# Moving one activation tile by 448 bytes and running three short passes once, in a two-layer encoder trunk

## The chip, the cores and the metric

The kernel runs on one core of one Trainium2 chip. The metric is the device time of one execution in microseconds. Before the change the median of three runs is 2716.47 us (2715.73 to 2719.71).

## The reference, cut to what matters

The trunk takes 256 tokens of width 2048 and puts 16 learned tokens ahead of them. Layer 0 is a state-space mixer and a SwiGLU feed-forward; then one shared K and V is projected; layer 1 is a stick-breaking attention and a second SwiGLU feed-forward; a final norm follows and the 16 tokens are dropped. Everything is float32. The part that the change touches is this:

```python
def swiglu(u, w_gate_up, w_down):
    gu = u @ w_gate_up
    return (jax.nn.silu(gu[..., :FFN_HIDDEN]) * gu[..., FFN_HIDDEN:]) @ w_down
...
h = h + swiglu(rmsnorm(h, norm_ffn[layer]), ffn_gate_up[layer], ffn_down[layer])
```

FFN_HIDDEN is 5632, so a feed-forward multiplies by a 2048 x 11264 and a 5632 x 2048 matrix. In layer 1 only the 256 tokens that are returned go through it.

## The kernel before

**How the work is tiled.** Activations lie transposed: 128 partitions carry 128 features, the free dimension carries tokens, and a tensor of width 2048 is 16 blocks k. Each output tile of 128 features by 256 (or 272) tokens is one accumulation in a PSUM bank over all k. TensorE holds a 128x128 piece of the weight matrix and streams the tokens of block k past it.

**Three passes for one product.** Each float32 operand is split into two float32r halves, a rounded one and the remainder. ScalarE casts the rounded weights `hi` (line 101), VectorE subtracts to get `lo` (line 103). `mac` (lines 107 to 112) then issues three passes per k: hi with the rounded activation (line 110), hi with the activation's remainder (111), lo with the rounded activation (112). A pass is one load of a 128x128 weight piece into the array and one matmul; the weights are loaded anew for each pass.

**Activation tiles.** A tile such as `u` has the shape [128, 16, 2, tokens]: for each k the rounded half and then the remainder. With 256 tokens each half is 1024 bytes per partition, so all halves of a tile begin at the same distance from a multiple of 512 (and of 1024). In the program as it is allocated the second feed-forward's input `u` (made at line 596 in a slot that the inputs of the earlier stages used before it) begins at byte 26,624 of each partition, which is 52 x 512. The query projection's input `uq` begins at 126,400, which is 246 x 512 + 448, the output projection's input `ob` at 159,168 (310 x 512 + 448), and the second feed-forward's hidden tile `hid` again at 126,400. All slots of `hi` and `lo` begin at multiples of 4096, and a 128x128 piece in them is 512 bytes per partition.

**Order of the work.** The order is written out by hand; each engine runs its own list, and semaphores connect them. `project` (line 114) makes one output tile in two halves of 8 k each: it issues the load of 512 KB of weights on SyncE's queue (five slots), the cast, the subtraction, and 24 passes. `project_block` (line 130) does the same for several output tiles at once, so that all of them run over the first 8 k before any needs the second 8.

**The second feed-forward.** `ffn` (line 472) makes the first four tiles (gate 0, up 0, gate 1, up 1) with `project_block`. Between its two halves stands `rstd` (line 165): one float32 matmul of the squared sums with a matrix of ones into the bank `pr`, a square root on ScalarE and a reciprocal on VectorE, which give the norm's factor `r`. Then the loop over 44 blocks m takes gate tile and up tile, from the four finished ones first and with `project` from m = 2 on; each is scaled by `r` (line 145), the gate goes through SiLU, the product is split into `hid`. The down projection follows: four tiles with `project_block`, twelve with `project`.

The lines around the tile are these; `finish_o` fills `u` while the attention's output projection runs, so the last matmuls on `ob` are followed directly by the first on `u`:

```python
u = upool.tile([P, KD, 2, SEQ], F32R, tag="u", name="u2")

def finish_o(m, ps):
    hm = h[:, m, META:]
    residual(hm, ps)
    split_scaled(u, m, hm, gam[:, 3, m:m + 1])
```

In the profile, u2 and the earlier tiles of that slot are all called u; those with 256 columns are u2.

Of the kernel before, what the change touches and what calls it, by code (L numbers as in the profile page):

```python
# [6 lines left out]
F32 = mybir.dt.float32  # L7
F32R = mybir.dt.float32r
# [5 lines left out]
P = 128  # L14
D = 2048
KD = D // P
SEQ = 256
# [25 lines left out]
def trunk(tc, a, out):  # L43
    nc = tc.nc
    V, S, PE = nc.vector, nc.scalar, nc.tensor

    with tc.tile_pool(name="const", bufs=1) as cp, \
# [38 lines left out]
        def nm(s):  # L86
            uid[0] += 1
            return f"{s}_{uid[0]}"


        def load(src, k0, n, m=P):
            raw = wp.tile([P, LC, P], F32, tag="raw", name=nm("raw"), bufs=RAW)
            b0 = k0 // LC * LC
            b1 = min(b0 + LC, src.shape[0] // (P * m))
            piece = src[b0 * P * m:b1 * P * m].rearrange("(p k c) -> p k c", p=P, c=m)
            nc.sync.dma_start(raw[:, :n, :m], piece[:, k0 - b0:k0 - b0 + n, :])
            return raw

        def halves(raw, n, m=P):
            hi = wp.tile([P, WC, P], F32R, tag="hi", name=nm("hi"), bufs=5)  # L100
            S.copy(hi[:, :n, :m], raw[:, :n, :m])  # L101
            lo = wp.tile([P, WC, P], F32R, tag="lo", name=nm("lo"), bufs=4)
            V.tensor_tensor(out=lo[:, :n, :m], in0=raw[:, :n, :m],  # L103
                            in1=hi[:, :n, :m].bitcast(F32), op=ALU.subtract)
            return hi, lo

        def mac(ps, hi, lo, j, x, k, first, last, m=P):
            n = x.shape[-1]
            wh, wl, xh, xl = hi[:, j, :m], lo[:, j, :m], x[:, k, 0, :], x[:, k, 1, :]
            PE.matmul(ps[:, :n], wh, xh, start=first, stop=False)  # L110
            PE.matmul(ps[:, :n], wh, xl, start=False, stop=False)  # L111
            PE.matmul(ps[:, :n], wl, xh, start=False, stop=last)  # L112

        def project(src, x, m=P, o=None, then=None):
            K = x.shape[1]
            if o is None:
                o = pp.tile([P, 512], F32, tag="pp", name=nm("pp"))
            o = o[:m]
            for k0 in range(0, K, WC):
                c = min(WC, K - k0)  # L120
                if k0 % LC == 0:
                    raw = load(src, k0, min(LC, K - k0), m)
                hi, lo = halves(raw[:, k0 % LC:], c, m)
                for j in range(c):
                    mac(o, hi, lo, j, x, k0 + j, k0 + j == 0, k0 + j == K - 1, m)
                if k0 == 0 and then:
                    then()
            return o

        def project_block(srcs, x, then=None):  # L130
            K = x.shape[1]
            pss = [pp.tile([P, 512], F32, tag="pp", name=nm("pp")) for _ in srcs]
            for k0 in range(0, K, WC):
                c = min(WC, K - k0)
                for ps, src in zip(pss, srcs):
                    hi, lo = halves(load(src, k0, c), c)
                    for j in range(c):
                        mac(ps, hi, lo, j, x, k0 + j, k0 + j == 0, k0 + j == K - 1)
                    pump()
                if k0 == 0 and then:  # L140
                    then()
            return pss

        def times(dst, ps, r):
            V.tensor_tensor(out=dst, in0=ps[:, :r.shape[-1]], in1=r, op=ALU.mult)  # L145
# [19 lines left out]
        def rstd(dst, acc, width, more=()):  # L165
            n = acc.shape[-1]
            ps = prp.tile([P, 512], F32, tag="pr", name=nm("pr"))
            parts = [acc, *more]
            for i, part in enumerate(parts):
                PE.matmul(ps[:, :n], ones, part, start=i == 0, stop=i == len(parts) - 1)  # L170
            sd = sp.tile([P, T], F32, tag="ms", name=nm("sd"), bufs=1)[:, :n]
            S.activation(sd, ps[:, :n], AF.Sqrt, bias=epst, scale=1.0 / width)
            V.reciprocal(dst, sd)
# [14 lines left out]
        u = upool.tile([P, KD, 2, T], F32R, tag="u", name="u0")  # L188
# [4 lines left out]
        for k, c in PIECES:  # L193
# [11 lines left out]
            hi, lo = halves(raw, GT * c)  # L205
# [6 lines left out]
        with tc.tile_pool(name="ssd0", bufs=1) as q0, \  # L212
# [13 lines left out]

            with tc.tile_pool(name="dtp", bufs=1) as dq:
                psd = project(a["w_dt"], u, m=NH, o=ptp.tile([P, 512], F32, tag="pt", name=nm("pt")),
                              then=lambda: rstd(rB, acc, D))[:, :T]
                for j in range(GT):  # L230
# [3 lines left out]
                def ahead(ct):  # L234
                    early[ct] = project(a["w_in"][32 + ct], u, o=pyp.tile([P, 512], F32, tag="py", name=nm("pe")))
# [37 lines left out]
                for b, (b0, b1) in enumerate(BLK):  # L273
                    n = b1 - b0
                    PE.transpose(pt[:n, b * NH:(b + 1) * NH], cum[:, b0:b1], ident[:NH, :NH])
                    PE.transpose(pt[:n, (3 + b) * NH:(4 + b) * NH], dt[:, b0:b1], ident[:NH, :NH])
                for b, (b0, b1) in enumerate(BLK):
                    n = b1 - b0
# [189 lines left out]
            u = upool.tile([P, KD, 2, T], F32R, tag="u", name="u1")  # L468
            out_project(6, u)


        def ffn(layer, u, t0, finish):
            n = T - t0
            with tc.tile_pool(name=f"ffn{layer}", bufs=1) as fp, \
                    tc.tile_pool(name=f"fft{layer}", bufs=2) as ft:
                hid = fp.tile([P, KF, 2, n], F32R, name=f"hid{layer}")
                gu, dn = a["w_gu"][layer], a["w_down"][layer]
                r = rB[:, t0:]
                pre = project_block([gu[0], gu[KF], gu[1], gu[KF + 1]], u,
                                    lambda: rstd(r, acc[:, t0:], D))  # L480
                for m in range(KF):
                    gt = ft.tile([P, n], F32, tag="gt", name=nm("gt"))
                    times(gt, pre.pop(0) if pre else project(gu[m], u), r)
                    S.activation(gt, gt, AF.Silu)
                    ut = ft.tile([P, n], F32, tag="ut", name=nm("ut"))
                    times(ut, pre.pop(0) if pre else project(gu[KF + m], u), r)
                    V.tensor_tensor(out=ut, in0=ut, in1=gt, op=ALU.mult)
                    S.copy(hid[:, m, 0, :], ut)
                    V.tensor_tensor(out=hid[:, m, 1, :], in0=ut, in1=hid[:, m, 0, :].bitcast(F32),
                                    op=ALU.subtract)  # L490
                for i, ps in enumerate(project_block([dn[m] for m in range(FILLERS)], hid)):
                    finish(i, ps)
                for m in range(FILLERS, KD):
                    finish(m, project(dn[m], hid))
# [3 lines left out]
        def finish0(m, ps):  # L498
# [4 lines left out]
            sumsq(acc, h[:, m, :], m == 0)  # L503

        ffn(0, u, 0, finish0)
        ukv = ukv[0]


        with tc.tile_pool(name="att1", bufs=1) as b1p, \
# [68 lines left out]
            pre = project_block([a["w_kv"][0], a["w_kv"][KD]], ukv, lambda: rstd(rB, acc, D))  # L578
# [14 lines left out]
                next(heads[m])  # L593
            side.extend(heads[-2:])

            u = upool.tile([P, KD, 2, SEQ], F32R, tag="u", name="u2")

            def finish_o(m, ps):
                hm = h[:, m, META:]
# [11 lines left out]
        def finish1(m, ps):  # L611
# [7 lines left out]
            if m == KD - 2:  # L619
                S.activation(warm, acc[:, META:META + 1], AF.Sqrt)  # L620

        ffn(1, u, META, finish1)


# [9 lines left out]
        pr = pp.tile([P, 512], F32, tag="pp", name="prow")  # L634
# [3 lines left out]
        m = 0  # L638
        for n in (1, 3, 4, 4, 4):
            o = wp.tile([P, LC, P], F32, tag="raw", name=nm("o"), bufs=RAW)  # L640
            o = o.rearrange("p k c -> p (k c)")[:, :n * SEQ].rearrange("p (k t) -> p k t", t=SEQ)
# [53 lines left out]
def build(shapes):  # L695
    import concourse.bacc as bacc

    nc = bacc.Bacc("TRN2", target_bir_lowering=False, num_devices=1, dynamic_dma_scratch_size=1024)
    a = {n: nc.dram_tensor(n, s, F32, kind="ExternalInput").ap() for n, s in shapes.items()}
    out = nc.dram_tensor("out", (P, KD, SEQ), F32, kind="ExternalOutput").ap()  # L700
    with tile.TileContext(nc) as tc:
        trunk(tc, a, out)
    return nc
# [11 lines left out]
```

## Time and profile before

| | |
|---|---|
| median of three runs | 2716.47 us |
| the profiled execution | 2715.76 us |
| its span | 2714.0 us |
| mean granted TensorE clock | 0.998 |
| TensorE busy, passes | 2700.6 us, 22112 |
| VectorE busy | 1605.6 us (59%) |
| ScalarE busy | 1307.1 us (48%) |
| DMA, mean | 177 GB/s |

The span runs from the first to the last instruction of one execution. Matmuls overlap: one that is listed with 280 ns begins some 115 ns after the one before it, so the pace of a stage is read from the starts or from the number of matmuls in a stretch of time, and not from the duration of one. A row of the grouped view has the line, the engine, the operation, the tile written and the tiles read, shapes, count, busy time in us and mean duration in ns; behind a second bar stands the idle time ahead of these instructions and what ended it. PE is TensorE's matmul, PEld its weight load, ACT ScalarE, DVE VectorE. In the row of a window stand its bounds in us, its length, the busy time and the number of instructions of the chosen engine, the granted clock, the DMA engines' busy share and GB/s.

### The profile page before, as it was taken

The page shows a single profiled execution, that of the slowest core. Times are in us where ns is not written, and L with a number is a line of the kernel's source. Part 1 is how long each engine was busy: PE and PEld are TensorE (multiplying, and loading weights), DVE is VectorE, ACT ScalarE, POOL GpSimd, SP SyncE. Part 2 cuts the span into 40 slices and gives each one's busy share as a digit, 9 for nine tenths or more (in the row PEclk, how much of TensorE's full clock was granted, in tenths as well). Part 3 has the DMA queues.
Part 4 walks back from the last instruction along what each step waited for, and adds up shares of the span by engine and source line. Part 5 has one row for each costly group of instructions (what it writes and reads, how often), then busy time and mean ns, then how long its engine had stood idle before and what let it go on. Part 6 is the DMA issues. An engine that isn't in the chain of part 4 may idle for free.

```text
span 2714.0 us, 52235 instructions
## 1 busy us (share of the span) xinstructions
PE 2700.6 (100%) x22112; PEld 2685.5 (99%) x22112; DVE 1605.6 (59%) x2220; ACT 1307.1 (48%) x1792; POOL 5.5 (0%) x22
## 2 busy tenths in 40 slices
PE   9999999999999999999999999999999999999998
PEld 9999999999999999999999999999999999999998
DVE  8777767668755555555444655555655555554554
ACT  7766566645544444444343544444544444443443
POOL 0000000000000000000000000000000000000000
PEclk9999999999999999999999999999999999999999
DMA  6755555654555555555555555555665666565664
GB/s 224 225 177 177 177 171 177 180 170 155 173 177 174 176 172 177 174 176 175 172 175 174 173 172 158 156 156 162 193 181 184 182 186 181 185 182 177 204 195 138
DMA packets 156235, 481.24 MB, mean 177 GB/s; under 512 B 18720, under 2 KB 39776, under 8 KB 156000
## 3 DMA queue, kind: packets, MB, share of 16 engines
q1 hardware_dynamic: 155712, 477.62, 57.3%
q8 instruction: 173, 2.83, 0.4%
q14 instruction: 62, 0.51, 0.1%
q10 hardware_dynamic: 288, 0.28, 0.0%
HBM read 475.67 MB, written 2.17 MB: 176 GB/s over the span
## 4 chain that ended last, share of the span: by engine, by line
PE 99%; DVE 0%; DMA 0%; ACT 0%; issue 0%; DVEq 0%; SPq 0%; ACTq 0%
PE pp L110 31%; PE pp L112 31%; PE pp L111 31%; PE py L422 1%; PE py L424 1%; PE pt L349 0%; PE po L571 0%; PE po L570 0%; PE psc L545 0%; PE pr L170 0%; DMA et<-cumD 0%; DMA raw<-w_first 0%; PE pe L110 0%; PE pe L112 0%; PE pe L111 0%; DVE o L642 0%
## 5 line engine op out<-in xcount | busy, mean ns | idle before, releaser
L101 ACT CAST hi<-raw 128x1024 fp32r<-128x1024 f32 (+1 forms) x899 | 928.5, 1034 | 1231.2 <-PE pp L111 994.9
L103 DVE TENSOR_TENSOR lo<-raw,hi 128x1024 fp32r<-128x1024 f32 (+1 forms) x899 | 1076.4, 1199 | 502.3 <-PE pp L112 280.9
L110 PE MATMUL pp<-u,hi 128*128 128x272 f32 (+1 forms) x4064 | 1166.7, 287 | 0.5 <-ACT hi L101 0.5
L112 PE MATMUL pp<-u,lo 128*128 128x272 f32 (+1 forms) x4064 | 1165.3, 287 | 0.2 <-DVE lo L103 0.2
L111 PE MATMUL pp<-u,hi 128*128 128x272 f32 (+1 forms) x4064 | 1163.2, 286 | 0.0
L111 PEld LDWEIGHTS pp<-u,hi 128*128 128x128 f32 x4064 | 775.3, 191 | 0.2
L110 PEld LDWEIGHTS pp<-u,hi 128*128 128x128 f32 x4064 | 769.4, 189 | 1.2 <-ACT hi L101 0.7
L112 PEld LDWEIGHTS pp<-u,lo 128*128 128x128 f32 x4064 | 768.9, 189 | 1.2 <-DVE lo L103 0.8
L110 PE MATMUL pp<-hid,hi 128*128 128x272 f32 (+1 forms) x1408 | 397.0, 282 | 0.0
L112 PE MATMUL pp<-hid,lo 128*128 128x272 f32 (+1 forms) x1408 | 396.4, 282 | 0.0
L111 PE MATMUL pp<-hid,hi 128*128 128x272 f32 (+1 forms) x1408 | 396.1, 281 | 0.0
L111 PEld LDWEIGHTS pp<-hid,hi 128*128 128x128 f32 x1408 | 265.3, 188 | 0.0
L110 PEld LDWEIGHTS pp<-hid,hi 128*128 128x128 f32 x1408 | 264.6, 188 | 0.0
L112 PEld LDWEIGHTS pp<-hid,lo 128*128 128x128 f32 x1408 | 264.3, 188 | 0.0
L110 PE MATMUL pp<-ukv,hi 128*128 128x272 f32 x512 | 149.0, 291 | 0.0
L110 PE MATMUL pp<-y,hi 128*128 128x272 f32 x512 | 148.7, 290 | 0.0
L112 PE MATMUL pp<-ukv,lo 128*128 128x272 f32 x512 | 147.6, 288 | 0.0
L111 PE MATMUL pp<-y,hi 128*128 128x272 f32 x512 | 147.4, 288 | 0.0
L111 PE MATMUL pp<-ukv,hi 128*128 128x272 f32 x512 | 147.4, 288 | 0.0
L112 PE MATMUL pp<-y,lo 128*128 128x272 f32 x512 | 147.1, 287 | 0.0
L145 DVE TENSOR_TENSOR gt<-pp,rB 128x272 f32<-128x272 f32 (+1 forms) x88 | 38.1, 433 | 145.0 <-PE pp L112 145.0
L145 DVE TENSOR_TENSOR ut<-pp,rB 128x272 f32<-128x272 f32 (+1 forms) x88 | 38.1, 433 | 144.0 <-PE pp L112 144.0
(218 smaller groups left out, 2602.2 us busy)
## 6 DMA issues: line engine op xcount, KB each, us to landing
raw<-w_gu SPq DMA_DIRECT2D x352, 512.0 KB, 3.6
raw<-w_down SPq DMA_DIRECT2D x160, 512.0 KB, 3.8
raw<-w_in SPq DMA_DIRECT2D x152, 512.0 KB, 3.6
raw<-w_out SPq DMA_DIRECT2D x64, 512.0 KB, 3.7
raw<-w_kv SPq DMA_DIRECT2D x64, 512.0 KB, 3.6
raw<-w_q SPq DMA_DIRECT2D x32, 512.0 KB, 3.6
raw<-w_o SPq DMA_DIRECT2D x32, 512.0 KB, 3.6
raw<-w_down SPq DMA_DIRECT2D x32, 256.0 KB, 2.6
```

What stands on the lines that cost most here:

```text
L101: S.copy(hi[:, :n, :m], raw[:, :n, :m])
L103: V.tensor_tensor(out=lo[:, :n, :m], in0=raw[:, :n, :m], in1=hi[:, :n, :m].bitcast(F32), op=ALU.subtract)
L110: PE.matmul(ps[:, :n], wh, xh, start=first, stop=False)
L111: PE.matmul(ps[:, :n], wh, xl, start=False, stop=False)
L112: PE.matmul(ps[:, :n], wl, xh, start=False, stop=last)
L145: V.tensor_tensor(out=dst, in0=ps[:, :r.shape[-1]], in1=r, op=ALU.mult)
L422: PE.matmul(py[i * HD:(i + 1) * HD, c0:c1], xd[b][:, 2 * j + i, :], gm[b][:, 2 * j + i, :], start=b < 2, stop=b != 1)
L424: PE.matmul(py[:, T:T + T - OQ], xw[:, 2 * j:2 * j + 2, :], cb[:, OQ:T], start=True, stop=True)
```

## The change

The tile u2 is made 112 float32r elements (448 bytes) longer, and the kernel uses what lies behind these 112 elements, in the same shape as before. All halves of u2 thus begin 448 bytes past a multiple of 512, 64 bytes short of the next one. And `project` gets a hook that is called when the first half's `hi` and `lo` exist, ahead of its first pass. It is used once, in the second feed-forward for the gate tile of m = 2, which is the fifth output tile that is made there: three passes of 128 columns (hi with the rounded activation, hi with the remainder, lo with the rounded activation, all of k = 0) write the bank `pr`, and nobody reads what they write.

```diff
-        def project(src, x, m=P, o=None, then=None):
+        def project(src, x, m=P, o=None, then=None, before=None):
...
                 hi, lo = halves(raw[:, k0 % LC:], c, m)
+                if k0 == 0 and before:
+                    before(hi, lo)
                 for j in range(c):
                     mac(o, hi, lo, j, x, k0 + j, k0 + j == 0, k0 + j == K - 1, m)
...
+        def syncopate(x):
+            def short(hi, lo):
+                b = prp.tile([P, 512], F32, tag="pr", name=nm("beat"))
+                for w, s in ((hi, 0), (hi, 1), (lo, 0)):
+                    PE.matmul(b[:, :P], w[:, 0, :], x[:, 0, s, :P], start=True, stop=True)
+            return short
...
-                    times(gt, pre.pop(0) if pre else project(gu[m], u), r)
+                    beat = syncopate(u) if (layer, m) == (1, 2) else None
+                    times(gt, pre.pop(0) if pre else project(gu[m], u, before=beat), r)
...
-            u = upool.tile([P, KD, 2, SEQ], F32R, tag="u", name="u2")
+            u = upool.tile([P, 112 + KD * 2 * SEQ], F32R, tag="u", name="u2")
+            u = u[:, 112:].rearrange("p (k s n) -> p k s n", k=KD, s=2)
```

## The prediction

> **What bounds the kernel now.** I read the page first: the span, the busy line and the chain of waits.
>
> ```profile
> span 2714.0 us, 52235 instructions
> ...
> PE 2700.6 (100%) x22112; PEld 2685.5 (99%) x22112; DVE 1605.6 (59%) x2220; ACT 1307.1 (48%) x1792; POOL 5.5 (0%) x22
> ...
> PE 99%; DVE 0%; DMA 0%; ACT 0%; issue 0%; DVEq 0%; SPq 0%; ACTq 0%
> ```
>
> TensorE is busy all the way and is 99% of the chain, so nothing but the pace of its passes (one weight load and one matmul each) can move the end by much. A pass's own duration overlaps its neighbours', so the pace has to be counted. I did that by stage, in the view that sums windows (the x is the number of passes touching the window, two or three of them begun before it):
>
> ```profile
> 1970.00:2460.00 490.00, 490.00 (x4085) 1.00 0.60 183
> 2463.00:2700.00 237.00, 237.00 (x2094) 1.00 0.59 179
> 1880.00:1950.00 70.00, 70.00 (x620) 1.00 0.62 191
> ```
>
> The first window is the second feed-forward's gate and up projection (moving tile u), the second its down projection (hid), the third the attention's output projection (ob). All three stream 256 columns against 128x128 weights at a granted clock of 1.00 (the column ahead of the DMA share), yet a pass costs 490/4083 = 120.0 ns in the first and 237/2092 = 113.3 ns and 70/618 = 113.3 ns in the others. The grouped view shows the same two kinds of pass:
>
> ```profile
> L110 PE MATMUL pp<-u,hi 128*128 128x256 f32 x1408 | 398.6, 283 | 0.0
> L110 PE MATMUL pp<-hid,hi 128*128 128x256 f32 x704 | 194.3, 276 | 0.0
> ...
> L111 PEld LDWEIGHTS pp<-u,hi 128*128 128x128 f32 x1361 | 261.3, 192 | 0.0
> ...
> L111 PEld LDWEIGHTS pp<-hid,hi 128*128 128x128 f32 x698 | 131.0, 188 | 0.0
> ```
>
> With u both the matmul (283 against 276 ns) and the weight load (192 against 188) take longer, with no idle time ahead of the load. What differs is the address: u stands at 0 modulo 512 bytes, the others (and the query input uq) at 448, while every weight slot stands at 0; each operand is 1024 bytes, so these distances hold for every pass of a stage. I read it as weight loads and matmuls that read the on-chip memory together and hold each other up when both start at the same place in it; this is an inference, the trace shows only that three tiles at 448 reach 113.3 and the one at 0 does not.
>
> Single rows give the stage's exact ends, which the sum needs:
>
> ```profile
> 1954.89 0.28 PE L112 MATMUL pp<-ob,lo 128*128 128x256 f32 x1
> 1955.00 0.28 PE L110 MATMUL pp<-u,hi 128*128 128x256 f32 x1
> ...
> 1966.50 0.59 PE L170 MATMUL pr<-acc,ones 128*128 128x256 f32 x2
> 1966.75 0.47 PE L110 MATMUL pp<-u,hi 128*128 128x256 f32 x1
> 1967.05 0.28 PE L111 MATMUL pp<-u,hi 128*128 128x256 f32 x1
> ...
> 1978.44 0.28 PE L110 MATMUL pp<-u,hi 128*128 128x256 f32 x1
> ...
> 2462.28 0.29 PE L110 MATMUL pp<-hid,hi 128*128 128x256 f32 x1
> ...
> 2462.64 0.28 PE L110 MATMUL pp<-hid,hi 128*128 128x256 f32 x1
> ...
> 2701.55 0.28 PE L112 MATMUL pp<-hid,lo 128*128 128x256 f32 x1
> ```
>
> The columns are start and duration in us. The stage lasts 2462.28 - 1955.00 = 507.28 us. The norm's reduction at 1966.50 costs 0.25 us itself and makes the next interval 0.30 instead of 0.12, so 0.43 us in all; the 88 x 16 x 3 = 4224 passes take 506.85, or 120.0 ns each. Down's 2111 intervals take 239.27 us, 113.34 ns each.
>
> **The pace is a rhythm that is entered, and 448 has two of them.** This is what the three short passes are about, so I looked for the slow stretches at 448:
>
> ```profile
> 1555.67 0.28 PE L110 MATMUL pp<-uq,hi 128*128 128x256 f32 x1
> ...
> 1561.21 0.28 PE L112 MATMUL pp<-uq,lo 128*128 128x256 f32 x1
> ...
> 1595.13 0.28 PE L111 MATMUL pp<-uq,hi 128*128 128x256 f32 x1
> ...
> 1600.36 0.28 PE L112 MATMUL pp<-uq,lo 128*128 128x256 f32 x1
> ...
> 1867.12 0.38 PE L572 MATMUL po<-ab,vb 128*128 128x128 f32 x2
> ...
> 1867.46 0.28 PE L111 MATMUL pp<-ob,hi 128*128 128x256 f32 x1
> ...
> 1870.05 0.28 PE L112 MATMUL pp<-ob,lo 128*128 128x256 f32 x1
> ```
>
> The first head's 48 query passes, entered straight from 272-column ones, run at 5.54/47 = 117.9 ns to their end. Those of a later head, entered from the attention's small matmuls, need 5.23/46 = 113.7 with the first few passes in it. And 23 passes on ob, entered from the same kind of small matmuls (the row at 1867.12), run at 2.59/22 = 117.7. So at 448 a stretch falls into 113.3 or into about 117.8, depending on how it is entered, and none changes by itself before something interrupts it. In all I count 22 entries at 448 (16 heads, five runs on ob, one on hid): 19 ended at 113.3, three at 117.8. Fifteen of the 19 are one and the same sequence, so this is weaker than it looks.
>
> **The change, part by part.**
>
> *The shift.* The tile grows by 448 bytes to 33,216, below the 34,816 that this slot already has for the first layer's inputs, so nothing else moves. The writers of u (line 151) write the same elements. Its direct worth is 4224 x (120.0 - 113.33) = 28.17 us, if the fast rhythm holds throughout. Entry: the passes on ob run on into u without a stop (1954.89 is the last, 1955.00 the first), and after the change both have the same distances to the weights, so 113.3 should simply go on. Then the reduction interrupts; its row is kept at 0.43. Should the 96 passes between it and the short passes be slow, that is 96 x 4.4 ns = 0.43 us, which I leave to the range.
>
> *The three short passes.* They stand ahead of the first matmul of the fifth tile (1978.44 before, about 1.3 us earlier after). No row shows a 128-column pass of this type. From below, half of a 256-column pass, 0.06; the nearest rows are the attention's transposes, 128 columns with a weight load each:
>
> ```profile
> 1600.47 0.27 PE L560 MATMUL pa<-ident,sc 128*16 128x128 f32 x1
> ...
> 1601.23 0.27 PE L537 MATMUL pt<-ident,vT 128*128 128x128 f32 x1
> ```
>
> From the first to the eighth there are seven intervals in 0.76 us, 0.109 each. From above I take a full start from rest, the 0.30 of the row after the reduction. So 0.18 to 0.9 us for three; I take 3 x 0.109 = 0.33, since a short pass still brings its whole weight load. They wait for nothing new: they read the hi and lo slots that the fifth tile's first three passes would read at once after them, and the bank they write was last read by the activation at 1968.95:
>
> ```profile
> 1968.95 0.47 ACT L172 ACTIVATE sd<-pr,epst 128x256 f32<-128x256 f32 x1
> ```
>
> That is nine microseconds of cover. Without it, with the short passes right behind the reduction, TensorE and the whole projection queued behind them would stand until that read's end: 1969.42 - 1966.75 = 2.7 us. No DMA is added, and the weight slots are released 0.33 us later, once.
>
> *Can the suppliers follow a faster TensorE?* The grouped view of the stage has their two operations:
>
> ```profile
> L103 DVE TENSOR_TENSOR lo<-raw,hi 128x1024 fp32r<-128x1024 f32 x171 | 208.6, 1220 | 61.7 <-issue 57.9
> L101 ACT CAST hi<-raw 128x1024 fp32r<-128x1024 f32 x171 | 179.8, 1052 | 237.5 <-PE pp L111 171.2 <-issue 65.0 <-PE pp L112 0.7
> ```
>
> A 24-pass group will take 2.72 us instead of 2.88. ScalarE's cast of it takes 1.05 and VectorE's difference 1.22, and ScalarE mostly waits for a slot that TensorE has yet to free (171.2 of 237.5 us idle). The weights' transfers rise from 183 to 183 x 120/113.3 = 194 GB/s; ob at that pace drew 191 without a stall. I cost this at nothing; if a group came late, ScalarE or the queue would show as what ended TensorE's idle time.
>
> *The down projection* keeps its address. Before, its first intervals were settling (three took 2462.64 - 2462.28 = 0.36 us instead of 0.34); afterwards it takes over u's rhythm. In the forecast that is worth nothing.
>
> *Sum.* 4224 x 0.11333 = 478.72, + 0.43 + 0.33 + 0.03 for settling after the two interruptions = 479.51 us, against 507.28: -27.8. The profiled execution took 2715.76 us, 1.76 over its span, so 2715.76 - 27.8 = **2688.0 us** and a span of 2686.2. The median of the three runs shown, 2716.47, is 0.7 above that execution; the runs' median could lie as much above.
>
> **The rivals.**
>
> *The short passes end in the slow rhythm, in this stage alone.* The 4032 passes behind them gain 120.0 - 117.8 = 2.2 ns instead of 6.67: 8.9 us, with 1.3 from the first 192, less 0.4: 2706.0. For it: the three slow entries above. Against it: the other 19. Neither kind was entered from short passes of this type, so the count is all I have.
>
> *The same, and hid inherits it.* Nothing interrupts between u and hid, and after the change no address does either; before, the step from 0 to 448 was what restarted the rhythm. Then down pays 2112 x (117.8 - 113.34) = 9.4 us, which eats the gain: 2715.4.
>
> *Slower.* The same inheritance with the 120 rhythm: if 120 belongs to the way in (the reduction, then the short passes) and not to the address, u keeps it from the fifth tile on and hands it to hid, which so far shook it off at the change of address. Price 2112 x 6.66 = 14.1, plus 0.35, less 1.3 for the first tiles: 2728.9. The point from which this decides: 4032 x (120 - p) + 930 = 2112 x (p - 113.34), p = 117.9 ns; any shared rhythm above that loses. Against it: in 22 entries at 448 none stayed at 120.
>
> *The address does nothing* and u stays at 120 with hid as before: 2715.76 + 0.33 = 2716.1. For it: only one stage is slow, so stage and address can't be told apart there. Against it: uq, ob and hid are three stages with different work around them and one pace. The Trainium skill, "SBUF — State Buffer" (Who interferes with whom), speaks for this rival: it gives TensorE two independent read ports, one for the moving operand and one for weights, and says that "PE and ACT never wait on anyone". By that rule the shift is worth nothing; the trace, where load and matmul are both longer at one address (192 and 283 against 188 and 276 ns), disagrees with it as far as one stage can.
>
> **How the numbers follow.** Forecast 0.68; slow in this stage alone 0.12; slow and inherited 0.07; address does nothing 0.05; slower 0.08. Forecast and first rival together hold 0.80, so the range runs from 2685 (short passes at their lower bound, a little run-to-run spread, and a rhythm as quick as the transposes' for part of the stage) to 2707. 0.2% is 5.4 us, about what a measurement of this kernel can tell from no change: faster 0.80, same 0.12 (inherited slow rhythm, address without effect), slower 0.08.
>
> **What would show it.** Right: the u matmuls at 276 ns and their loads at 188, a start every 0.113 us right after 1955.0 and again within some ten passes of the short ones, hid at 276 as before, stage length 479.5. The short passes right: a row of three from the new function's line about 0.11 apart. Slow rhythm: matmuls between 276 and 283 ns and 117.8 a pass behind the short ones, and in hid too if inherited. Wrong altogether: 283 and 120 with u at 448. Suppliers late: idle time of TensorE put down to the hi or lo line.

## The result

The changed kernel is faster by 1.0%. In the first comparison three of its executions took 2688.45, 2691.48 and 2692.06 us against a median of 2716.11 before, a ratio of 0.9903 (95% interval 0.989 to 0.9917); in a second one, with 22 executions of the kernel before, 2688.36 us (2687.9 to 2688.84) against 2715.91, a ratio of 0.9896 (0.9883 to 0.991). One execution of the first comparison, the one that was profiled, ran with a mean granted TensorE clock of 0.208 and took 12,094 us; it is left out everywhere, and the profile after is that of the second comparison. Forecast were 2688.0 us and a range of 2685 to 2707.

The page of the changed kernel (second comparison; this execution took 2688.09 us):

```profile
span 2686.4 us, 52240 instructions
...
PE 2672.8 (99%) x22115; PEld 2657.6 (99%) x22115; DVE 1602.9 (60%) x2220; ACT 1307.6 (49%) x1792; POOL 5.5 (0%) x22
...
PE 99%; DVE 0%; DMA 0%; ACT 0%; issue 0%; SPq 0%; DVEq 0%
```

TensorE still bounds everything; it has three passes more and is busy for 28 us less. Here is where the time went, first by windows (bounds, length, TensorE's busy time and the passes that touch the window, granted clock, DMA share, GB/s): the attention's output projection on ob, the gate and up projection on u, the down projection on hid.

```profile
1900.00:1950.00 50.00, 50.00 (x444) 1.00 0.64 195
1990.00:2440.00 450.00, 450.00 (x3973) 1.00 0.63 194
2475.00:2660.00 185.00, 185.00 (x1634) 1.00 0.62 191
```

With two passes taken off that began before the window, a pass on u costs 450/3971 = 113.3 ns instead of 120.0, and ob and hid are where they were. (From 2434 on the second window already counts hid, at the same pace.) The rows of u in the grouped view of that window say the same for a single instruction: 276 ns a matmul and 188 a load, as hid had before.

```profile
L110 PE MATMUL pp<-u,hi 128*128 128x256 f32 x1307 | 360.9, 276 | 0.0
...
L112 PEld LDWEIGHTS pp<-u,lo 128*128 128x128 f32 x1307 | 245.4, 188 | 0.0
```

Then the timeline of TensorE (start and duration in us), from the stage's first pass to hid's:

```profile
1954.30 0.28 PE L110 MATMUL pp<-u,hi 128*128 128x256 f32 x1
...
1965.18 0.59 PE L172 MATMUL pr<-acc,ones 128*128 128x256 f32 x2
1965.43 0.47 PE L110 MATMUL pp<-u,hi 128*128 128x256 f32 x1
1965.73 0.28 PE L111 MATMUL pp<-u,hi 128*128 128x256 f32 x1
1965.85 0.28 PE L112 MATMUL pp<-u,lo 128*128 128x256 f32 x1
...
1976.80 0.28 PE L112 MATMUL pp<-u,lo 128*128 128x256 f32 x1
1976.92 0.33 PE L478 MATMUL beat<-u,hi 128*128 128x128 f32 x2
1977.09 0.28 PE L478 MATMUL beat<-u,lo 128*128 128x128 f32 x1
1977.20 0.34 PE L110 MATMUL pp<-u,hi 128*128 128x256 f32 x1
...
1978.19 0.28 PE L112 MATMUL pp<-u,lo 128*128 128x256 f32 x1
...
1978.87 0.28 PE L112 MATMUL pp<-u,lo 128*128 128x256 f32 x1
...
2434.24 0.28 PE L110 MATMUL pp<-hid,hi 128*128 128x256 f32 x1
```

The first 96 passes take 1965.18 - 1954.30 = 10.88 us, 113.3 ns each, as on ob before them. Behind the reduction it is different: from 1965.85 to 1976.80 there are 93 intervals, 10.95/93 = 117.7 ns. Then come the three short passes, and from 1978.19 to 1978.87 six intervals take 0.68 us, 113.3 ns again, which holds to the end of hid. The stage lasts 2434.24 - 1954.30 = 479.94 us instead of 507.28.

### The profile page after: what moved, and what is told of

Its sections match the earlier page's. It is cut to its first block, busy times and chain, and to the rows that moved or that the text cites. A ratio compares the mean times of both kernels' runs of the same rounds, so it can differ in the third digit from the quotient of the medians.

```text
span 12092.4 us, 52240 instructions
## 1 busy us (share of the span) xinstructions
PE 12080.0 (100%) x22115; PEld 11996.6 (99%) x22115; DVE 1609.1 (13%) x2220; ACT 1322.0 (11%) x1792; POOL 5.5 (0%) x22
## 4 chain that ended last, share of the span: by engine, by line
PE 100%; DMA 0%; DVE 0%; ACT 0%; SPq 0%; issue 0%; DVEq 0%; ACTq 0%
PE pp L112 32%; PE pp L110 32%; PE pp L111 32%; PE psc L556 0%; PE po L581 0%; PE po L582 0%; PE psc L555 0%; PE py L424 0%; PE po L583 0%; PE pr L172 0%; PE py L426 0%; PE pt L351 0%; PE pt L547 0%; PE pb L574 0%; PE pb L575 0%; PE pt L548 0%
## 5 line engine op out<-in xcount | busy, mean ns | idle before, releaser
L110 PE MATMUL pp<-u,hi 128*128 128x272 f32 (+1 forms) x4064 | 3331.3, 820 | 0.8 <-ACT hi L101 0.8
L112 PE MATMUL pp<-u,lo 128*128 128x272 f32 (+1 forms) x4064 | 3328.1, 819 | 0.0
L111 PE MATMUL pp<-u,hi 128*128 128x272 f32 (+1 forms) x4064 | 3325.4, 818 | 0.0
L111 PEld LDWEIGHTS pp<-u,hi 128*128 128x128 f32 x4064 | 2869.4, 706 | 0.9 <-issue 0.8
L110 PEld LDWEIGHTS pp<-u,hi 128*128 128x128 f32 x4064 | 2865.9, 705 | 2.3 <-ACT hi L101 1.6
L112 PEld LDWEIGHTS pp<-u,lo 128*128 128x128 f32 x4064 | 2864.8, 705 | 0.6 <-DVE lo L103 0.2
L110 PE MATMUL pp<-hid,hi 128*128 128x272 f32 (+1 forms) x1408 | 1484.1, 1054 | 0.0
L111 PE MATMUL pp<-hid,hi 128*128 128x272 f32 (+1 forms) x1408 | 1483.2, 1053 | 0.0
L112 PE MATMUL pp<-hid,lo 128*128 128x272 f32 (+1 forms) x1408 | 1483.0, 1053 | 0.0
L111 PEld LDWEIGHTS pp<-hid,hi 128*128 128x128 f32 x1408 | 1316.1, 935 | 0.0
L112 PEld LDWEIGHTS pp<-hid,lo 128*128 128x128 f32 x1408 | 1316.0, 935 | 0.0
L110 PEld LDWEIGHTS pp<-hid,hi 128*128 128x128 f32 x1408 | 1315.7, 934 | 0.0
L110 PE MATMUL pp<-ukv,hi 128*128 128x272 f32 x512 | 557.2, 1088 | 0.0
L111 PE MATMUL pp<-ukv,hi 128*128 128x272 f32 x512 | 549.8, 1074 | 0.0
L110 PEld LDWEIGHTS pp<-ukv,hi 128*128 128x128 f32 x512 | 469.9, 918 | 2.6 <-issue 2.6
L111 PEld LDWEIGHTS pp<-ukv,hi 128*128 128x128 f32 x512 | 470.4, 919 | 0.4 <-issue 0.4
```

## The experiments

All start from the changed kernel. A diff is shown against it; windows are read as above.

**The changed kernel again.** No edit.

> The changed kernel once more, for a profile at full clock. Both theories: a gate and up stage of 479.5 us with u at 113.3 ns a pass and hid at 113.3, about 2688. Three undisturbed runs so far gave 2688.45, 2691.48 and 2692.06; if these are two rhythms and not noise, some stretch of 3 us worth stands at another pace in the profile of a run near 2691.5: 3.2 us over 4.4 ns is about 730 passes, or 1450 at 2.2 ns.

2688.36 us, the profile shown above. No execution of this set was near 2691.5, so the second half of the expectation had to wait for other runs (below, on ob).

**The shift alone.**

```diff
-                    beat = syncopate(u) if (layer, m) == (1, 2) else None
+                    beat = None
```

> u at 448, without the three short passes. Address theory (the address sets the pace, the way in only decides between two rhythms, and the reduction's restart happens to lead to the fast one): 113.3 ns to the end, 0.33 us less than the changed kernel, 2687.7. Rival, the short passes are what brings the fast rhythm: the 4128 passes behind the reduction stay at 117.8 and gain 2.2 ns each, 2706; with hid inheriting the slow rhythm, 2715.

2715.28 us (eleven executions, 2714.37 to 2718.87), ratio 0.9997 (0.9988 to 1.0006): without the short passes the shift gains nothing. The windows of ob, u and hid:

```profile
1900.00:1950.00 50.00, 50.00 (x443) 1.00 0.64 192
1990.00:2440.00 450.00, 450.00 (x3823) 1.00 0.61 187
2475.00:2660.00 185.00, 185.00 (x1573) 1.00 0.60 185
```

u goes at 450/3821 = 117.8 and hid at 185/1571 = 117.8 ns, where hid had 113.3 in both kernels so far. This is the rival in which the slow rhythm is handed on, and its figure, 2715.4. u gains some 9.8 us and hid pays 9.4. The grouped view of the same stretch of u shows what a pass looks like in this rhythm:

```profile
L112 PE MATMUL pp<-u,lo 128*128 128x256 f32 x1275 | 358.5, 281 | 0.0
...
L112 PEld LDWEIGHTS pp<-u,lo 128*128 128x128 f32 x1274 | 244.7, 192 | 0.0
L111 PEld LDWEIGHTS pp<-u,hi 128*128 128x128 f32 x1274 | 239.2, 188 | 0.0
L110 PEld LDWEIGHTS pp<-u,hi 128*128 128x128 f32 x1274 | 239.2, 188 | 0.0
```

One of the three loads has the 192 ns that all have at 120.0, two have the 188 of the fast rhythm: a turn of three passes that repeats.

**The short passes alone**, u back at 0 modulo 512.

```diff
-            u = upool.tile([P, 112 + KD * 2 * SEQ], F32R, tag="u", name="u2")
-            u = u[:, 112:].rearrange("p (k s n) -> p k s n", k=KD, s=2)
+            u = upool.tile([P, KD, 2, SEQ], F32R, tag="u", name="u2")
```

> The three short passes with u back at 0 modulo 512. Address theory: u stays at 120.0 ns on both sides of the short passes, 2715.8 + 0.33 = 2716.1. Rival, the way in sets the rhythm whatever the address: u at 113.3 behind the short passes, 2689 or so.

2716.45 us, ratio 1.0003 (0.9993 to 1.0012): the address theory's figure. Neither part of the change gains anything alone.

```profile
1900.00:1950.00 50.00, 50.00 (x427) 1.00 0.59 184
1990.00:2440.00 450.00, 450.00 (x3753) 1.00 0.60 183
2475.00:2660.00 185.00, 185.00 (x1635) 1.00 0.62 191
```

u is at 450/3751 = 120.0 and hid at 113.3: at 0 the short passes change nothing, and hid, at 448, starts afresh behind u as it did before. The first row is new: in this execution, which took 2718.93 us, ob went at 50/425 = 117.6 instead of 113.3. (One pass more or less in 425 is 0.3 ns; by the starts of its 672 passes it is 117.8, the slow rhythm.) I come back to it.

**Other distances.** The shift is made 64, 192 and 128 bytes (16, 48 and 32 elements in place of 112), short passes kept.

> The changed kernel with the tile shifted by 64 bytes and not 448. If only the distance to 512 on the one side counts (a start shortly ahead of the weights' place), 64 behind is another case and u stays near 120: 2716. If any start that differs from the weights' by 64 bytes or more does, 113.3 and 2688. In between, a pace p: 2715.8 + 0.33 - 4.224 x (120 - p) us.

> The changed kernel with a shift of 192 bytes, which is 448 less one 256. The stages with 272 columns repeat their paces with a period of 256 bytes in the start, so if the on-chip memory conflicts have that period: the same as at 448, 117.8 behind the reduction, 113.3 behind the short passes, u stage 479.9 us, 2688. If the distance to the next 512 counts: some other pace, 117.8 (stage 498) or 120 (507).

> The changed kernel with a shift of 128 bytes. So far 0 gives 120.0, 64 gives 117.8, 192 and 448 give 117.8 or 113.3. If the hold-up shrinks with the distance from the weights' start and 192 is the only distance with a fast rhythm: 117.8 or 120 here, 2706 to 2716. If it is a matter of lying at least two lines of 64 bytes off: 113.3 behind the short passes, 2688.

64 bytes: 2706.78 us, ratio 0.9966 (0.9954 to 0.9979). 192 bytes: one execution, 2688.66. 128 bytes: one execution, 2710.51. The window of u of each, in this order, the first with hid's:

```profile
1990.00:2440.00 450.00, 450.00 (x3824) 1.00 0.61 187
2475.00:2660.00 185.00, 185.00 (x1635) 1.00 0.62 192
```

```profile
1990.00:2440.00 450.00, 450.00 (x3973) 1.00 0.62 194
```

```profile
1990.00:2440.00 450.00, 450.00 (x3795) 1.00 0.59 185
```

At 64 the pace is 117.7 and the short passes don't change it; hid, at another distance, is back at 113.3. This is not the reduction's doing: the 96 passes ahead of the reduction, entered from ob at 113.3, go from 1954.32 to 1965.63, 117.8 ns each. At 192 everything is as at 448, which a period of 256 bytes would give. At 128 it is 450/3793 = 118.6 behind the short passes, a pace that none of the expectations had. And 128 has two paces, as the starts in that run show (the stage's first pass, the reduction, the third pass behind it, the last one ahead of the short passes):

```profile
1954.90 0.29 PE L110 MATMUL pp<-u,hi 128*128 128x256 f32 x1
...
1966.29 0.59 PE L172 MATMUL pr<-acc,ones 128*128 128x256 f32 x2
...
1966.95 0.28 PE L112 MATMUL pp<-u,lo 128*128 128x256 f32 x1
...
1978.12 0.29 PE L112 MATMUL pp<-u,lo 128*128 128x256 f32 x1
```

The first 96 passes take 11.39 us, 118.6 ns each; behind the reduction 93 intervals take 11.17 us, 120.1 each; behind the short passes it is 118.6 again. So at 128, too, the stage came out of the reduction at a slower pace and out of the short passes at the faster one, only closer together. The work, the bytes and the order are the same in all of these runs and every other tile stays where it was; only the start of u differs, and behind the short passes it gives 120.0 (0), 117.7 (64), 118.6 (128) and 113.3 (192 and 448).

**How many short passes, and must they be short?** One (hi with the rounded half) or two in place of three; and three of 256 columns.

```diff
-                for w, s in ((hi, 0), (hi, 1), (lo, 0)):
+                for w, s in ((hi, 0),):
...
-                    PE.matmul(b[:, :P], w[:, 0, :], x[:, 0, s, :P], start=True, stop=True)
+                    PE.matmul(b[:, :SEQ], w[:, 0, :], x[:, 0, s, :], start=True, stop=True)
```

> The changed kernel with one short pass (hi with the rounded half) in place of three. If any short pass lets the next weight load get ahead of its matmul and so re-enters the rhythm, 113.3 behind it, 2688 less 0.22. If the slow rhythm repeats every three passes and it takes a whole turn of three to leave it, 117.8 remains and hid inherits it: 2715.4.

> Two short passes (hi with both halves) in place of three, u at 448. One changed nothing (117.8 went on into hid), three ended at 113.3. If each short pass brings the weight loads forward a little and a threshold must be passed: either way, 113.3 (2688) if two suffice, 117.8 and hid inheriting it (2715.5) if not. If the number must be a whole turn of the three kinds of pass: 117.8, 2715.5.

> The three extra passes with all 256 columns in place of 128. If it is their shortness that breaks the slow rhythm: 117.8 goes on behind them, hid inherits it, 2715.3 + 0.35 = 2715.6. If any interruption or change of weights does it: 113.3 and 2688.

One execution each: 2715.59 us with one short pass, 2692.36 with two, 2719.26 with three full ones. The windows of u and hid with one:

```profile
1990.00:2440.00 450.00, 450.00 (x3823) 1.00 0.60 187
2475.00:2660.00 185.00, 185.00 (x1573) 1.00 0.58 185
```

of ob, u and hid with two:

```profile
1900.00:1950.00 50.00, 50.00 (x427) 1.00 0.59 187
1990.00:2440.00 450.00, 450.00 (x3973) 1.00 0.62 195
2475.00:2660.00 185.00, 185.00 (x1635) 1.00 0.61 193
```

and with three full ones:

```profile
1900.00:1950.00 50.00, 50.00 (x427) 1.00 0.60 187
1990.00:2440.00 450.00, 450.00 (x3823) 1.00 0.59 187
2475.00:2660.00 185.00, 185.00 (x1573) 1.00 0.57 183
```

Two short passes are enough, one is not, and three full ones are not: the passes have to be short to leave the slow rhythm, and no turn of three is needed. The last two times lie 3.7 us above 2715.6 and 2688.7; ob, in the slow rhythm in both, and the first 96 passes of u that take its pace over account for (672 + 96) x 4.4 ns = 3.4 us of it.

The one short pass did leave a trace, in the loads behind it:

```profile
L111 PEld LDWEIGHTS pp<-u,hi 128*128 128x128 f32 x1274 | 244.8, 192 | 0.0
...
L112 PEld LDWEIGHTS pp<-u,lo 128*128 128x128 f32 x1274 | 239.2, 188 | 0.0
```

Ahead of the short pass the 192 ns are those of line 112, as in the shift alone; behind it they are those of line 111. Every third load stays the long one, with the short pass counted among them. So the long load belongs to a place in the turn of three and not to `lo`, and one short pass only moved it on by one place.

**Without the reduction.** The shift alone, and the norm's reduction left out.

```diff
-                                    lambda: rstd(r, acc[:, t0:], D))
+                                    None if layer else lambda: rstd(r, acc[:, t0:], D))
...
-                    beat = syncopate(u) if (layer, m) == (1, 2) else None
+                    beat = None
```

> The shift alone, with the norm's reduction left out of the second feed-forward (its factor r is then an older one, so that part of the computation is missing: one float32 matmul, a root and a reciprocal). If the reduction is what throws the stage into 117.8: ob's 113.3 runs on through u and hid without any short pass, 4224 x 0.11333 = 478.7 us for u, in all about 2687.3. If u at 448 falls into 117.8 in another way (the switch of banks between its first tiles, the faster drain of the weights): 2706 to 2715.

2687.38 us, one execution.

```profile
1990.00:2440.00 450.00, 450.00 (x3973) 1.00 0.62 194
2475.00:2660.00 185.00, 185.00 (x1634) 1.00 0.59 191
```

113.3 through u and hid with no short pass at all. With the timeline of the changed kernel, where the pace goes from 113.3 to 117.7 at the reduction, this shows that the interruption by the reduction throws the stage into the slow rhythm, and that the short passes are needed because of it. (Whether its float32 matmul does it or the stop around that, this can't tell.)

**Can the same be had for 272 columns?** The earlier inputs in this slot have halves of 1088 bytes, which walk through all distances. Here each half is given 1280.

```diff
-RAW = 5
+RAW = 4
...
+        def padded(name):
+            t = upool.tile([P, 64 + KD * 2 * 320], F32R, tag="u", name=name)
+            return t[:, 48:48 + KD * 2 * 320].rearrange("p (k s n) -> p k s n", k=KD, s=2)[:, :, :, :T]
...
-        u = upool.tile([P, KD, 2, T], F32R, tag="u", name="u0")
+        u = padded("u0")
...
-            u = upool.tile([P, KD, 2, T], F32R, tag="u", name="u1")
+            u = padded("u1")
...
-                ukv[0] = upool.tile([P, KD, 2, T], F32R, tag="u", name="ukv")
+                ukv[0] = padded("ukv")
```

> The changed kernel with the three earlier 272-column inputs of this slot padded, so that every half begins 1280 bytes after the one before it and 192 past a multiple of 256 (the weights' raw slots go from five to four to make room, everything else keeps its distance modulo 256). 9504 passes are concerned, at 125.5 ns now. If their pace is the same hold-up at starts that walk through all distances: 16 columns more than the fast 113.3 at 0.417 ns each, 120.0 ns, 9504 x 5.5 = 52 us less, 2636. If 272 columns fall into a slow rhythm at this distance, 120.0 + 4.4 = 124.4: 2678. If the distance doesn't bear on 272 columns, or four slots don't suffice: 2688 or more.

2668.98 us (2667.68 to 2672.01), ratio to the kernel before 0.9827 (0.9809 to 0.9844). The window lies in the first feed-forward's gate and up projection; first the kernel before, then this one with its window on ob:

```profile
780.00:1230.00 450.00, 450.00 (x3586) 1.00 0.57 175
```

```profile
780.00:1230.00 450.00, 450.00 (x3651) 1.00 0.56 178
1880.00:1930.00 50.00, 50.00 (x427) 1.00 0.58 184
```

From 450/3584 = 125.6 to 450/3649 = 123.3 ns, and not to 120.0. If all 9504 passes gained as much it would be some 21 us, and the median is 19.4 below the changed kernel's 2688.36. Both expectations (120.0 and 124.4) missed the pace, and with it the time (2636 and 2678). The raw slots went from five to four in the same edit; what that does alone was not run. This version beats both kernels.

**Short passes in two more places**, on the padded kernel.

```diff
-                    beat = syncopate(u) if (layer, m) == (1, 2) else None
+                    beat = syncopate(u) if m == 2 else None
...
-                finish_o(m, project(a["w_o"][m], ob))
+                finish_o(m, project(a["w_o"][m], ob, before=syncopate(ob) if m == FILLERS else None))
```

> The padded kernel with three short passes in two more places: ahead of the fifth gate and up tile of the first feed-forward, and ahead of the fifth tile on ob. On ob, which now goes at 113.3 in some executions and at 117.8 in others: if the short passes lead to the fast rhythm from either, 113.3 behind them always, and the executions near 2672 (3 us above the others) are gone. In the first feed-forward, now at 123.3 behind its reduction: if that is a slow rhythm with a fast one beside it at 120.0, 4032 x 3.3 = 13.4 us less, 2655; if 123.3 is the only rhythm of 272 columns at this distance, 0.33 more, 2669.

2669.59 us (2669.32 to 2670.94), ratio 0.983 (0.9817 to 0.9844), no difference to the padded kernel that these runs can tell.

```profile
780.00:1230.00 450.00, 450.00 (x3651) 1.00 0.58 178
1880.00:1930.00 50.00, 50.00 (x443) 1.00 0.65 196
```

The first feed-forward stays at 123.3, behind its reduction as well as behind the short passes, so no second rhythm of 272 columns was found at this distance. On ob it is inconclusive: none of the five executions was near 2672, but that is too few, and the profiled one went at 113.3 on ob before the short passes as well as behind them.

## Why the prediction was right, and where its steps were not

**The sum.** 479.51 us were forecast for the stage and 479.94 measured. The difference is the term that I named and left to the range: the 96 passes between the reduction and the short passes did fall into the slow rhythm, 96 x 4.4 ns = 0.42. The end of ob handed its 113.3 to u, as expected. From 1976.92 to 1978.19 there are three short passes and eight others; 1.27 - 8 x 0.1133 = 0.36 us for the short ones and the settling, against 0.33 + 0.01. The suppliers followed: 194 GB/s, as worked out, with TensorE never idle in the stage.

**What each part was worth.** Here the reasoning fell short. I put the whole 28.17 us on the shift ("its direct worth") and the short passes down as a cost of 0.33 us and one more way in. In truth neither is worth anything alone (2715.28 and 2716.45 us): the shift makes a fast rhythm possible, the reduction loses it, and the short passes bring it back. I counted 22 entries, 19 of them into 113.3, and gave 0.68; but the entry behind this reduction led to 117.8 in all eight profiles that have it with u at 448 or 192, and none of the eleven executions of the shift alone came within 22 us of any of the changed kernel's. The count mixed ways in that have little to do with each other. (Of its fifteen heads at 113.3, fourteen come from the same place, the row of line 572; the second head is entered from line 545.) No entry in it was from short passes of this type, as the prediction said itself, so that these lead to the fast rhythm was a bet on a weak base, and that it came out was luck.

**The rivals.** "The same, and hid inherits it" did not happen in the changed kernel, but the inheritance and its price are what the shift alone shows: 2715.4 worked out, 2715.28 measured; one short pass gives the same, 2715.59. "The address does nothing" has fallen: with everything else equal the four distances give four paces. The rule of the Trainium skill, "SBUF — State Buffer" (Who interferes with whom), by which TensorE's two read ports are independent and it never waits on anyone, spoke for it; by that rule the shift was worth nothing, and the runs show 120.0 against 113.3 ns a pass. My own reading, loads and matmuls that hold each other up, is not shown by this. At 0 both are longer (192 and 283 ns against 188 and 276), but at 64 and 128, behind the short passes, the loads keep 187 to 188 ns and only the matmuls are longer, 279 to 282. Nor did the weights ever leave the multiples of 256, so the distance to the weights and the place of u by itself are not told apart. The rival on the other side, a shared rhythm above 117.9, was not seen; the shared one that was seen, 117.8, lies right at that point, and the time was the same as before.

**What I missed.** I took ob's 113.3 from one profile. In four of the thirteen profiles at full clock ob goes at 117.8 instead, through its last 672 passes, and this accounts for the 3 us by which some executions of most of these kernels stand above the others: 672 passes x 4.4 ns = 3.0 us. In such an execution u at 448 starts slow too, 96 x 4.4 ns more, 3.4 us in all: 2688.1 + 3.4 = 2691.5. The executions at 2691.48 and 2692.06 fit that, and so does the one with two short passes (2692.36), whose window shows ob slow; for the first two, which have no profile, it is only argued.

## What to carry to other kernels

Where TensorE reloads weights for every pass, count passes in a window, stage by stage, with equal shapes beside each other: a stage that is a few per cent slower at a granted clock of 1.00 and without idle time may differ in the address of its moving tile alone, and moving it a few hundred bytes cost nothing here, where the slot had the room. Then look again behind each interruption, since the pace there can be another one and is carried on from tile to tile until something breaks it. Judge two such edits together and apart; here each alone would have been thrown away.

## What the runs showed of the hardware

- The pace of a 256-column pass with a 128-column weight load depends on where the moving tile starts: with the weights at multiples of 256 bytes, 120.0 ns at 0 modulo 256, 117.7 at 64, 118.6 or 120.1 at 128, 113.3 or 117.8 at 192 (a shift of 192 and one of 448 gave the same; in the padded kernel the weight slots stand 2304 bytes, nine times 256, further on, and u kept its 117.8 and 113.3). That loads and matmuls meet in the on-chip memory is my reading of it; no run looked inside.
- The pace is a state. At 448 it stayed at 117.8 through some 6000 passes, across tiles, slots and the change from u to hid, and two 128-column passes moved it to 113.3, where it stayed as long. One such pass and three 256-column ones didn't, in one execution each. In the 117.8 rhythm every third load takes 192 ns instead of 188, whichever operand it loads.
- A short pass is not half a pass: the timeline has two in 0.17 us and the third in 0.11, and with what the next passes lose the three cost 0.36 us, about 0.12 each, as much as full ones.
- Which rhythm ob falls into differs between profiles of programs that are the same up to there, and the times argue that it differs between executions of one program, while the entry behind the reduction was slow in all eight profiles. Why, stays open, and so does why 272 columns settle at 123.3.
